# Batched matmul on one core: the seventh of eight output groups stored by two engines, in strided and uneven transfers

## The chip, the core and the metric

The kernel runs on one core of one Trainium2 chip. The metric is the device time of one execution in microseconds, as a median over runs. A profile of one execution stands beside it; its span goes from the first to the last instruction.

## The reference

```python
def setup_inputs():
    batch, dim_i, dim_j, dim_k = 32, 256, 512, 384
    ...  # x: [32, 256, 512] float32, y: [32, 512, 384] float32, normal draws

def reference(x, y):
    return np.einsum('bij,bjk->bik', x, y).astype(np.float32)
```

So there are 32 independent products of a 256x512 by a 512x384 matrix. x has 16.8 MB, y 25.2 MB, the output 12.6 MB.

## The kernel before

The batch is worked in N = 8 groups of Q = 4 matrices. On chip a group lies on all 128 partitions: matrix g has partitions 32g to 32g+31, and each partition holds R = 8 consecutive rows of x and of the output. Below, "row" means such a partition row of the output: 8 x 384 float32 = 12,288 bytes, contiguous in memory on both sides, 128 of them to a group. A group is computed in NE = 2 halves (the first and last four of the eight matrix rows of each partition).

The engines share the work of a group like this.

- SyncE (`sp`) issues every DMA. First the loads: `load_y` (L73) and `load_x` (L69) bring a group of y (3,072 KB) or x (2,048 KB) into one of two buffers; for groups 2 to 7 each load waits until GpSimd has converted the group two before it. Then the stores, all through `store` (L96): groups 0 to 4 in one DMA, groups 5 and 6 in a second, group 7 in a third. All outputs stay in `o_sb`, which has room for all eight groups, so no computation waits for a store.
- GpSimd (`po`) converts x and y to float16: `round_x` (L126), `round_y` (L136). Its last conversions are those of group 7. After them it waits for SyncE's `s_sp` and clears the semaphores.
- VectorE (`v`) transposes 32x32 blocks of the converted x (L156) and copies five of sixteen result blocks of each half from PSUM to `o_sb` (L165).
- TensorE (`te`) multiplies (L217), in four row groups of the array.
- ScalarE (`a_`) copies the other eleven result blocks of each half (L165).

The store part of SyncE's program:

```python
    sp.wait_ge(s_pe, chunk_done(JOINED, NE - 1, 0))
    store(0, JOINED)                 # groups 0 to 4
    sp.wait_ge(s_pe, chunk_done(N - 1, NE - 1, 0))
    store(JOINED, N - 1)             # groups 5 and 6
    sp.wait_ge(s_act, NE)
    sp.wait_ge(s_dve, NE)
    store(N - 1, N)                  # group 7
```

`s_pe` is counted up by TensorE; `chunk_done(n, e, a)` is its value when chunk a of half e of group n has been multiplied. That of the last half of group 7 can only be reached when the results of group 6 have been copied out, so the second store is safe there. The last lines of the program wait until all stores have landed.

Of the kernel before, what the change touches and what calls it, by code (L numbers as in the profile page):

```python
# [10 lines left out]
P = 128  # L11
Q = 4
NE = 2
STEP = 4
STRAIGHT = 2
JOINED = 5
# [3 lines left out]
def kernel(  # L20
# [6 lines left out]
    nc = tc.nc  # L27
# [4 lines left out]
    PQ = P // Q  # L32
    R = I // PQ
# [3 lines left out]
    N = B // Q  # L37
    NC = T // STEP

    def sbuf(name, shape, dtype):  # L40
        return nc.alloc_sbuf_tensor(name, shape, dtype).ap()
# [3 lines left out]
    o_sb = sbuf("o_sb", [P, N, NE, H, K], F32)  # L45
# [6 lines left out]
    s_x = [nc.alloc_semaphore(f"s_x{n}") for n in range(N)]  # L52
    s_y = [nc.alloc_semaphore(f"s_y{n}") for n in range(N)]
    s_xt = nc.alloc_semaphore("s_xt")
    s_yr = nc.alloc_semaphore("s_yr")
    s_cast = nc.alloc_semaphore("s_cast")
    s_free = nc.alloc_semaphore("s_free")
    s_act = nc.alloc_semaphore("s_act")
    s_dve = nc.alloc_semaphore("s_dve")
    s_pe = nc.alloc_semaphore("s_pe")  # L60
    s_sp = nc.alloc_semaphore("s_sp")
    s_out = nc.alloc_semaphore("s_out")
    mine = s_x + s_y + [s_xt, s_yr, s_cast, s_free, s_act, s_dve, s_pe, s_sp]
    nums = sorted(s.num for s in mine)
    assert nums == list(range(nums[0], nums[-1] + 1)) and s_out.num == nums[-1] + 1

# [21 lines left out]
    def chunk_done(n, e, a):  # L88
        return (n * NE + e) * MARKS + (a + 1 if a < NC - 1 else MARKS)

    sp = nc.sync

    def store(first, last):
        groups = out[first * Q : last * Q].rearrange("(n g) (s f) k -> (g s) n f k", g=Q, s=PQ)
        src = o_sb[:, first:last].rearrange("p n e h k -> p n (e h) k")
        sp.dma_start(out=groups, in_=src).then_inc(s_out, 16)  # L96

    for n in range(2, N):
# [3 lines left out]
        load_y(n)  # L102
    sp.wait_ge(s_pe, chunk_done(JOINED, NE - 1, 0))
    store(0, JOINED)
    sp.wait_ge(s_pe, chunk_done(N - 1, NE - 1, 0))
    store(JOINED, N - 1)
    sp.wait_ge(s_act, NE)
    sp.wait_ge(s_dve, NE)
    store(N - 1, N)
    sp.sem_inc(s_sp, 1)  # L110
    sp.wait_op(s_out, 16 * 3, "sem-ge").then_inc(s_out, -16 * 3)

    def pieces(n):
        w = 1 if n in (0, N - 2, N - 1) else 2
        return [(a, a + w) for a in range(0, NC, w)]

    po = nc.gpsimd

    def round_x(n):
        po.wait_ge(s_x[n], 16)
        for e in range(NE):
            if n:
                po.wait_ge(s_free, max(2 * n - 2 + e, 1))
            po.tensor_copy(  # L126
                x_r[:, e], x_sb[n % 2][:, e * H : (e + 1) * H]
            ).then_inc(s_cast, 1)

    def round_y(n):  # L130
        po.wait_ge(s_y[n], 16)
        for a, b in pieces(n):
            if n:
                po.wait_ge(s_pe, chunk_done(n - 1, NE - 1, b - 1))
            s = slice(a * STEP, b * STEP)
            ins = po.tensor_copy(y_r[:, s], y_sb[n % 2][:, s])  # L136
            ins.then_inc(s_yr, b - a if b < NC else b - a + NC)
# [3 lines left out]
    for n in range(1, N):  # L141
        round_x(n)
        round_y(n)
    po.wait_ge(s_sp, 1)
    po.sem_clear(range(nums[0], nums[-1] + 1))

# [84 lines left out]
    with te.Fori(0, N):  # L231
        with te.Fori(0, NE) as e:
            take(s_act)
            take(s_dve)
            for t in range(T):
# [3 lines left out]
                for g in range(Q):  # L239
                    s = slice(g * PQ, (g + 1) * PQ)  # L240
# [40 lines left out]
```

## Time and profile before

| | |
|---|---|
| median of 3 runs | 131.91 us (131.77 to 132.49) |
| the profiled execution, its own time | 132.13 us |
| its span | 130.8 us |
| bytes moved | 54.55 MB, mean 417 GB/s over the span |
| busy: PE, DVE, ACT, POOL | 61.4, 82.7, 84.1, 74.2 us |
| DMA transfers issued | 19: 16 loads and 3 stores, all by SyncE |

The profile's page gives busy times of the five compute engines and, apart from them, what the core's 16 DMA engines did: a row with their mean busy share in 40 equal slices of the span, and the rate in each slice. A DMA is cut into packets, and each of the 16 engines works its own packets one after the other. In this kernel a packet of a store is one row of 12,288 bytes, and every DMA ends with one small packet on each engine, which counts up its semaphore. The trace names no engine for a packet.

### The profile page before, as it was taken

Reading aid. Unit: us, or ns where it says so; the run is one execution under the profiler, and the core shown is the slowest. Engines: PE = TensorE matmul, PEld = TensorE weight load, DVE = VectorE, ACT = ScalarE, POOL = GpSimd, SP = SyncE. Lnnn points to the kernel's source line nnn. Section 1 sums busy time; section 2 is a strip of 40 time slices with the busy share of each in tenths; the row PEclk is TensorE's granted clock in tenths of the full one; section 3 lists DMA queues with packets and bytes.
Section 4 is the critical chain, followed back from the end, with each engine's and each line's share of the span. In section 5 each row is a group of like instructions: output and inputs, shape, how many; then the busy total and the mean of one; then the engine's idle time right before and its main releaser. Section 6 shows DMA issues by size and latency. Waiting matters only on the chain. (4 is left out here: it accounts for less than half of the span.)

```text
span 130.8 us, 3199 instructions
## 1 busy us (share of the span) xinstructions
PE 61.4 (47%) x1024; PEld 46.7 (36%) x1024; DVE 82.7 (63%) x144; ACT 84.1 (64%) x178; POOL 74.2 (57%) x42
## 2 busy tenths in 40 slices
PE   0000009910992589089329905980975499100000
PEld 0000009800991566046129604970953236000000
DVE  0000036899379999985997997599999957920000
ACT  0400000599659989993998899399999957994000
POOL 0006991199929965992899459758973970000000
PEclk9999999995589689977986985599599959965555
DMA  5999999999999999999999999999999999999995
GB/s 120 451 396 441 421 431 451 443 408 428 451 413 421 438 443 401 436 436 443 423 458 398 443 408 466 398 418 436 463 398 408 427 438 425 436 428 421 425 440 248
DMA packets 3379, 54.55 MB, mean 417 GB/s; under 512 B 304, under 2 KB 304, under 8 KB 304
## 3 DMA queue, kind: packets, MB, share of 16 engines
q1 hardware_dynamic: 3376, 54.53, 98.1%
q14 instruction: 3, 0.02, 0.0%
HBM read 41.94 MB, written 12.58 MB: 417 GB/s over the span
## 5 line engine op out<-in xcount | busy, mean ns | idle before, releaser
L165 ACT COPY o_sb<-o_ps (+1 forms) x176 | 82.6, 469 | 31.7 <-PE o_ps L217 29.6
L217 PE MATMUL o_ps<-y_r,xt_sb 32*128 32x384 f16 x1024 | 61.4, 384 | 50.4 <-PEq L214 49.5
L217 PEld LDWEIGHTS o_ps<-y_r,xt_sb 32*128 32x128 f16 x1024 | 46.7, 107 | 64.6 <-issue 56.8
L156 DVE STREAM_TRANSPOSE xt_sb<-x_r 128x256 f32<-128x256 f32 x64 | 38.1, 626 | 30.9 <-POOL x_r L126 18.4
L136 POOL CAST y_r<-y_sb 128x1536 f16<-128x1536 f32 (+1 forms) x22 | 44.3, 2049 | 15.8 <-DMA y_sb<-in_y_dram 15.3
L165 DVE COPY o_sb<-o_ps 32x384 f32 (+1 forms) x80 | 44.6, 557 | 1.6
L126 POOL CAST x_r<-x_sb 128x2048 f16<-128x2048 f32 x16 | 30.2, 1893 | 16.8 <-DVE o_sb L165 12.1
L202 ACT ACT_TABLE_LOAD x1 | 1.3, 1283 | 3.4 <-PEq L78 3.4
L265 POOL MEMSET const-float32-0.0<- 128x1 f32 x1 | 0.1, 98 | 0.2 <-issue 0.2
L202 ACT COPY spare<-const-float32-0.0 1x1 f32<-1x1 f32 x1 | 0.2, 190 | 0.0
L265 POOL MEMSET const-bfloat16-1.0<- 128x1 bf16 x1 | 0.1, 101 | 0.0
L265 POOL MEMSET const-uint8-127<- 128x1 uint8 x1 | 0.1, 101 | 0.0
L265 POOL MEMSET const-float32-1.0<- 128x1 f32 x1 | 0.1, 98 | 0.0
## 6 DMA issues: line engine op xcount, KB each, us to landing
y_sb<-in_y_dram SPq DMA_DIRECT2D x8, 3072.0 KB, 16.8
x_sb<-in_x_dram SPq DMA_DIRECT2D x8, 2048.0 KB, 17.0
out_dram<-o_sb SPq DMA_DIRECT2D x1, 7680.0 KB, 33.9
out_dram<-o_sb SPq DMA_DIRECT2D x1, 3072.0 KB, 17.3
out_dram<-o_sb SPq DMA_DIRECT2D x1, 1536.0 KB, 11.5
```

Of the source, the lines that this page charges most:

```text
L126: po.tensor_copy(x_r[:, e], x_sb[n % 2][:, e * H : (e + 1) * H]).then_inc(s_cast, 1)
L136: ins = po.tensor_copy(y_r[:, s], y_sb[n % 2][:, s])
L156: v.transpose(xt_w[:, w], words[:, e, w]).then_inc(s_xt, 1)
L165: ins = copy(o_sb[g * PQ : (g + 1) * PQ, n, e, h], o_ps[h * PQ : (h + 1) * PQ, e * Q + g, :K],)
L202: a_.copy(spare, nc.const_aps.tensor(0.0, [1, 1], F32))
L217: return te.add_instruction(mybir.InstMatmult(name=nc.get_next_instruction_name(), start_tensor_calc=start, stop_tensor_calc=stop, tile_si ...
L265: nc = _bacc.Bacc("TRN2", target_bir_lowering=False, num_devices=1)
```

## The change

Group 6 is no longer stored together with group 5. Group 5 gets a DMA of its own. Of group 6's 128 rows, SyncE stores 112 in three DMAs: every second row (64 rows), every fourth from row 1 (32 rows), every eighth from row 3 (16 rows). The other 16 rows, 7, 15, ... 127, are stored by GpSimd, in five DMAs, after its last conversion and after the same wait on `s_pe` that SyncE has. GpSimd's transfers are cut across the rows: some take matrix row 0 alone of each partition (1,536 bytes), some the matrix rows 1 to 7 (10,752 bytes).

| GpSimd's transfer | rows | matrix rows of each | bytes of each |
|---|---|---|---|
| first | 7 to 39 (5) | 0 | 1,536 |
| second | 47 to 127 (11) | 1 to 7 | 10,752 |
| third | 47 to 79 (5) | 0 | 1,536 |
| fourth | 7 to 39 (5) | 1 to 7 | 10,752 |
| fifth | 87 to 127 (6) | 0 | 1,536 |

SyncE waits for these five by a semaphore of their own, `s_few`, after it has issued the store of group 7. Computation is as before.

```diff
+    s_few = nc.alloc_semaphore("s_few")
...
+    def store_rows(eng, sem, n, first, step, f0=0, f1=R, rows=P):
+        dst = out[n * Q : (n + 1) * Q].rearrange("g (s f) k -> (g s) f k", s=PQ)
+        src = o_sb[:, n].rearrange("p e h k -> p (e h) k")
+        p = slice(first, min(first + rows * step, P), step)
+        eng.dma_start(out=dst[p, f0:f1], in_=src[p, f0:f1]).then_inc(sem, 16)
...
     sp.wait_ge(s_pe, chunk_done(N - 1, NE - 1, 0))
-    store(JOINED, N - 1)
+    store(JOINED, N - 2)
+    store_rows(sp, s_out, N - 2, 0, 2)
+    store_rows(sp, s_out, N - 2, 1, 4)
+    store_rows(sp, s_out, N - 2, 3, 8)
     sp.wait_ge(s_act, NE)
     sp.wait_ge(s_dve, NE)
     store(N - 1, N)
+    sp.wait_ge(s_few, 16 * 5)
     sp.sem_inc(s_sp, 1)
-    sp.wait_op(s_out, 16 * 3, "sem-ge").then_inc(s_out, -16 * 3)
+    sp.wait_op(s_out, 16 * 6, "sem-ge").then_inc(s_out, -16 * 6)
...
     for n in range(1, N):
         round_x(n)
         round_y(n)
+
+    po.wait_ge(s_pe, chunk_done(N - 1, NE - 1, 0))
+    store_rows(po, s_few, N - 2, 7, 8, 0, 1, 5)
+    store_rows(po, s_few, N - 2, 47, 8, 1, R, 11)
+    store_rows(po, s_few, N - 2, 47, 8, 0, 1, 5)
+    store_rows(po, s_few, N - 2, 7, 8, 1, R, 5)
+    store_rows(po, s_few, N - 2, 87, 8, 0, 1, 6)
     po.wait_ge(s_sp, 1)
```

More of the change, by code (lines that the diff above doesn't have):

```diff
@@ L61 @@
     s_sp = nc.alloc_semaphore("s_sp")
+    s_few = nc.alloc_semaphore("s_few")
     s_out = nc.alloc_semaphore("s_out")
-    mine = s_x + s_y + [s_xt, s_yr, s_cast, s_free, s_act, s_dve, s_pe, s_sp]
+    mine = s_x + s_y + [s_xt, s_yr, s_cast, s_free, s_act, s_dve, s_pe, s_sp, s_few]
     nums = sorted(s.num for s in mine)
```

## The prediction

> **What bounds the kernel now.** I read the page first, its time slices above all.
>
> ```profile
> span 130.8 us, 3199 instructions
> PE 61.4 (47%) x1024; PEld 46.7 (36%) x1024; DVE 82.7 (63%) x144; ACT 84.1 (64%) x178; POOL 74.2 (57%) x42
> DMA  5999999999999999999999999999999999999995
> DMA packets 3379, 54.55 MB, mean 417 GB/s; under 512 B 304, under 2 KB 304, under 8 KB 304
> q1 hardware_dynamic: 3376, 54.53, 98.1%
> q14 instruction: 3, 0.02, 0.0%
> ```
>
> No compute engine is busy for two thirds of the span, while the 16 DMA engines are busy in every slice but the first and the last, and 98.1% in all. So the bytes set the time. The row of queue 1 also counts packets: 304 small ones, which is 19 DMAs with one for each of 16 engines, and 3,072 large ones. Does a wait of SyncE ever leave the engines empty? The queue's waits and the issues answer that.
>
> ```profile
> SPq L96 <- PE o_ps L217: 24.9, 2, 23.5
> SPq L111 <- SPq L111: 11.1, 1, 11.1
> 109.82 9.80 SPq L96 DMA_DIRECT2D out_dram<-o_sb  x2
> L96 SPq DMA_DIRECT2D out_dram<-o_sb x3: 345/390/403, 85.9 to 119.3; - x3
> out_dram<-o_sb SPq DMA_DIRECT2D x1, 7680.0 KB, 33.9
> out_dram<-o_sb SPq DMA_DIRECT2D x1, 3072.0 KB, 17.3
> out_dram<-o_sb SPq DMA_DIRECT2D x1, 1536.0 KB, 11.5
> ```
>
> The first store is issued at 85.9 us and lands 33.9 us later, at 119.8. The second goes out at 109.82, ten microseconds before that; the third at 119.27, and lands at 130.8, the end. Each is in the queue before the one ahead of it is done, so the engines never run dry; SyncE's waits cost nothing, and its last wait, 11.1 us, is for the bytes.
>
> Next the rate, by stage, from the windows.
>
> ```profile
> core 0: us, PE busy (x) PEld busy (x) DVE busy (x) ACT busy (x) POOL busy (x), PEclk, DMA share, GB/s
> 4.00:97.00 93.00, 50.41 (x835) 40.76 (x835) 67.15 (x117) 64.01 (x137) 66.37 (x33) 0.85 1.01 431
> 109.80:119.00 9.20, 1.94 (x46) 1.19 (x37) 5.21 (x10) 8.96 (x20) 0.00 (x0) 0.79 1.01 431
> 119.00:127.00 8.00, 0.00 (x0) 0.00 (x0) 0.00 (x0) 0.25 (x1) 0.00 (x0) 0.50 0.99 424
> ```
>
> Loads and stores run at the same 431 GB/s, 26.9 GB/s for each of 16 engines. One row of 12,288 bytes therefore holds an engine for 12,288 / 26.9 = 456 ns. That is the unit of all that follows. Nothing in the change removes a byte, so only the last stretch, where engines finish one by one, can give anything back. Here are the DMA packets from 129.0 us on, in 40 slices of 50 ns.
>
> ```profile
> DMA  9550005959000000500000000000000000000000
> GB/s 983 246 246 0 0 0 246 738 246 492 0 0 0 0 0 0 246 0 0 0 0 0 0 0 0 0 0 0 0 0 0 0 0 0 0 0 0 0 0 0
> DMA packets 30, 0.17 MB, mean 86 GB/s; under 512 B 16, under 2 KB 16, under 8 KB 16
> ```
>
> A packet is entered where it starts, and 246 GB/s for 50 ns is 12.3 KB, one row. So the numbers are counts: 4, 1, 1 rows start from 129.00 to 129.15, then 1, 3, 1, 2 from 129.30 to 129.50, and a single one at 129.80 to 129.85. (30 packets are these 14 rows and 16 small ones.) Each engine repeats every 456 ns. The seven after 129.30 belong to seven engines; the six before belong to six others or to two of these seven and four others, since one that starts at 129.00 starts again at 129.46. The two at the end of the second cluster (129.45 to 129.50) are such repeats, so four engines end near 129.5, the other five had started their last row before 129.0 and end by 129.46 (I take 129.3; all 16 small packets lie after 129.0, so none ended earlier), six end near 129.85, and one ends at 129.83 + 0.456 = 130.3, alone. The time from there to the landing at 130.8 is the same for all. So the kernel's end is set by one of 16 DMA engines, which is one row late.
>
> The mean end is (5 x 129.3 + 4 x 129.53 + 6 x 129.86 + 130.3) / 16 = 129.63. Perfect sharing would end 0.67 us earlier. This is the ceiling of any gain: 0.5% of the profiled time. About 0.5% is also what a measurement of this kernel can tell from no change (the three runs lie within 131.77 to 132.49).
>
> **The change part by part.** *Group 5 split off, and three strided DMAs.* SyncE issues four DMAs from 109.82 instead of one: at 390 ns each until 111.4, eight microseconds ahead of 119.27, when it issues group 7. Queued behind them is only that store, and it waits for the last copies anyway. Cost on SyncE: 0. If that cover were gone, 3 x 0.39 = 1.2 us.
>
> *Small packets.* Three more DMAs by SyncE and five by GpSimd add up to 8 small packets per engine. The two windows at 431 GB/s hold one DMA end in 9.2 us and some 15 in 93 us; within the rounding of the rate (0.5 in 431, 0.1 us of 93) the 15 cost at most 0.2 us, so one costs at most 14 ns. Eight: 0 to 0.11 us. I take 0.05.
>
> *GpSimd's issues.* Is GpSimd free?
>
> ```profile
> 104.15 2.88 POOL L136 CAST y_r<-y_sb 128x1536 f16<-128x1536 f32 x2
> L136 POOL CAST y_r<-y_sb x22: 1462/1467/2747, 10.9 to 105.6; 128x1536 f16<-128x1536 f32 x12, 128x3072 f16<-128x3072 f32 x10
> ```
>
> Its last conversion ends at 107.03, so its new wait ends at 109.8 as SyncE's does; behind it stands only the clearing of semaphores, which nobody waits for until the end. No DMA by GpSimd is in this trace. Its issue lies between SyncE's 0.345 us and its own longest instruction, 2.75 us: five take 1.7 to 13.7 us and end at 111.5 to 123.5. I take 1 us each, nearer to the row of the same operation, so 115. The 16 rows they move then still have 14 us. It would delay the end only if one transfer took (129.0 - 109.8) / 5 = 3.8 us. Cost 0. [...]
>
> *Who carries which bytes.* SyncE's 64, 32 and 16 rows divide by 16: 4 + 2 + 1 = 7 rows for each engine, where group 6 had 8. GpSimd's 16 rows would be one for each engine if spread evenly, but they are cut in 5, 11, 5, 5 and 6. The trace shows no such transfer. Bounds: an engine that gets none ends 0.456 us earlier; one that is first in all five transfers gets 3 x 1,536 + 2 x 10,752 = 26,112 bytes, 2.13 rows, and ends 1.13 x 0.456 = 0.51 us later. If the five transfers instead follow one another around the engines (5 + 11 and 5 + 5 + 6 are 16 each), five engines get 2 x 1,536 = 3,072 bytes and lose 0.75 row, 0.34 us; five get 2 x 10,752 bytes and gain 0.34 us; six keep 12,288 bytes. I take this second form for the size, since its three groups of 5, 5 and 6 are near the groups that the tail shows (5 early, 4 between, 7 late), and it lies between the bounds.
>
> [...]
>
> *Does that move the end?* The late engine ends at 130.3, the next at 129.93 (the last of the six, which starts its last row by 129.5). If the late one is relieved, the end falls by 0.34; if it is one of the six, it stays; if it is loaded, +0.34. With 0.05 for small packets: -0.29, +0.05, +0.39. Five engines end together early, and loading those costs nothing; then the late one is among the relieved or the untouched. I take the middle of these two, -0.1. Against the profiled 132.13 us that is 132.0; against the median 131.91, from which it is 0.22 away as runs differ, 131.8. The forecast case reaches from 131.6 (late engine relieved) to 132.2 (untouched, dearer small packets, part of a conflict below).
>
> **The rivals.** *Strided rows make engines get into each other's way.* Every DMA of the trace covers all 128 partitions, so no row shows what 16 engines do on every second, fourth or eighth partition. If two engines then read from the same part of the on-chip memory, and each row took 912 ns instead of 456, the seven rows of group 6 would cost 7 x 0.456 = 3.2 us on every engine: 135.1. If only the 16-row transfer is hit, 0.46 us; the 32 and 16 rows, 1.4 us; so 132.4 to 135.1. It decides from the point at which more than one of the seven rows doubles. For it: all engines run at the same 26.9 GB/s in loads and stores, as if something of a fixed width behind each were the limit. Against it: a stride of 2, 4 or 8 still reaches all of the partitions' range, and the limit may be the engine itself. 0.27 for over 0.5%.
>
> [...]
>
> *The wrong engines are loaded* (the change does not do what an uneven split is for): the late engine gets 0.34 to 0.51 us more, 132.3 to 132.5. For it: nothing in the trace says which engine is late; against it, 11 of 16 are not loaded. 0.14, and still within 0.5%.
>
> *GpSimd's DMAs disturb the engines*: a second queue makes each engine change over several times, or an issue takes over 3.8 us. Two to five stalls of about a row's time, 0.3 us, come to 0.7 to 1.5 us: 132.6 to 133.4. Against it: the three packets of queue 14 in the rows above went between those of queue 1 and the share stayed at 98.1%. 0.06.
>
> *All engines end together*, and the runs without a profile have a later straggler than this one: 0.67 us or more gained, 131.2 or less. A step of 0.34 us can't level a spread of 1 us. 0.06.
>
> **How the numbers follow.** Forecast 0.47, wrong engines 0.14: within 0.5%, 0.61. Strided conflicts 0.27 and disturbance 0.06: slower, 0.33. Faster 0.06. The range begins at 131.3, below the forecast's own 131.6 by half the 0.7 us over which the three runs lie, rounded to 0.3, and goes up to 134.0: it takes in the disturbance and all partial conflicts and leaves out the near full doubling (0.12) and most of the faster case (0.05).
>
> **What would show it.** Right: rows of group 6 still take 456 ns, so the rate stays near 431 GB/s from 109.8 to 127 us; group 7's store is issued at 119.3; GpSimd's issues end by 116 us and its rows land long before the end; the last rows start closer together than 129.0 to 129.85. Wrong: a stretch of several microseconds after 119 us at well under 431 GB/s (strided conflict), a slice between packets of the two queues with engines idle (disturbance), or two engines or more a row later than the others (wrong engines).

## The result: 0.6% slower, and the tail of one engine grew

The changed kernel took 132.77 us (median of 8 runs, 132.46 to 133.17), the kernel before 131.97 us beside it; the ratio is 1.0061, with a 95% interval of 1.0041 to 1.0081. So it is slower by 0.8 us, where 131.8 us was forecast. The profiled execution is one of the longer ones, 133.17 us with a span of 131.8 us.

Its page, the rows that answer those shown of before:

```profile
span 131.8 us, 3207 instructions
PE 65.4 (50%) x1024; PEld 52.5 (40%) x1024; DVE 82.4 (63%) x144; ACT 84.1 (64%) x178; POOL 76.7 (58%) x47
DMA  5999999999999999999999999999999999999993
DMA packets 3571, 54.55 MB, mean 414 GB/s; under 512 B 480, under 2 KB 496, under 8 KB 496
q1 hardware_dynamic: 3408, 54.33, 97.2%
q0 software_dynamic: 160, 0.20, 0.4%
q14 instruction: 3, 0.02, 0.0%
```

The bytes are the same, and the engines are as full as before, except in the last slice: 3 tenths instead of 5. A queue 0 has come in, with GpSimd's 0.20 MB. SyncE's waits and the issues, from the waits of the queue, GpSimd's timeline and the instructions that write the output:

```profile
SPq L124 <- SPq L124: 11.0, 1, 11.0
SPq L120 <- DVE o_sb L185: 1.8, 1, 1.8
SPq L123 <- DMA out_dram<-o_sb: 1.3, 1, 1.3
110.50 2.67 POOL L100 DMA_DIRECT2D out_dram<-o_sb  x5 [3.09 <-PE o_ps L237]
L100 POOL DMA_DIRECT2D out_dram<-o_sb x5: 518/518/636, 110.5 to 112.6; - x5
L105 SPq DMA_DIRECT2D out_dram<-o_sb x3: 337/350/407, 87.2 to 119.2; - x3
L100 SPq DMA_DIRECT2D out_dram<-o_sb x3: 758/870/949, 110.6 to 112.3; - x3
```

GpSimd's five issues end at 113.2, SyncE's strided ones at 113.3, and group 7's store still goes out at 119.2. SyncE's wait for GpSimd's rows takes 1.3 us and ends 11.0 us before the end. So nothing was issued late. The rates by stage, from the windows (columns as in the prediction; the last is GB/s):

```profile
109.80:119.00 9.20, 2.33 (x57) 1.30 (x48) 5.08 (x10) 8.96 (x20) 2.67 (x5) 0.91 1.01 426
119.00:127.00 8.00, 0.00 (x0) 0.00 (x0) 0.00 (x0) 0.13 (x1) 0.00 (x0) 0.50 1.02 428
127.00:129.00 2.00, 0.00 (x0) 0.00 (x0) 0.00 (x0) 0.00 (x0) 0.00 (x0) 0.50 0.98 418
```

Where GpSimd's rows move, the rate is 426 instead of 431 GB/s, which is 0.1 us of these 9.2; from 119 to 127 us it is 428, where it was 424 before. Most of the difference stands in the tail. The DMA packets from 129.0 us, in slices of 50 ns, where 246 GB/s is one row that starts:

```profile
DMA  9099590009559050009505500005500000000500
GB/s 737 0 492 737 246 492 0 0 0 737 246 246 983 0 246 0 0 0 492 246 0 246 246 0 0 0 0 246 246 0 0 0 0 0 0 0 0 246 0 0
DMA packets 44, 0.36 MB, mean 178 GB/s; under 512 B 15, under 2 KB 15, under 8 KB 15
```

Before, one row started after 129.5. Here eight rows start from 129.9 on; two of them at 130.35 to 130.45, one of whose engines starts yet another at 130.87 and ends at 131.33, where the last small packet stands. From that packet to the end of the span it is 0.5 us, as before from 130.30 to 130.8. One engine is now two rows or more behind most of the others. In this execution the last row starts 1.03 us later than before (130.87 against 129.85), a little more than the 0.8 us of the medians.

### The profile page after: what moved, and what is told of

Its sections match the earlier page's. It is cut to its first block, busy times and chain, and to the rows that moved or that the text cites. A ratio compares the mean times of both kernels' runs of the same rounds, so it can differ in the third digit from the quotient of the medians.

```text
span 131.8 us, 3207 instructions
## 1 busy us (share of the span) xinstructions
PE 65.4 (50%) x1024; PEld 52.5 (40%) x1024; DVE 82.4 (63%) x144; ACT 84.1 (64%) x178; POOL 76.7 (58%) x47
## 3 DMA queue, kind: packets, MB, share of 16 engines
q1 hardware_dynamic: 3408, 54.33, 97.2%
## 5 line engine op out<-in xcount | busy, mean ns | idle before, releaser
L237 PE MATMUL o_ps<-y_r,xt_sb 32*128 32x384 f16 x1024 | 65.4, 406 | 46.7 <-PEq L234 43.5
L237 PEld LDWEIGHTS o_ps<-y_r,xt_sb 32*128 32x128 f16 x1024 | 52.5, 113 | 59.2 <-issue 52.0
L100 POOL DMA_DIRECT2D out_dram<-o_sb x5 | 2.7, 542 | 3.1 <-PE o_ps L237 3.1
```

The lines of the kernel that those rows point to most:

```text
L100: eng.dma_start(out=dst[p, f0:f1], in_=src[p, f0:f1]).then_inc(sem, 16)
L237: return te.add_instruction(mybir.InstMatmult(name=nc.get_next_instruction_name(), start_tensor_calc=start, stop_tensor_calc=stop, tile_si ...
```

## The experiments

Theory A: GpSimd's transfers all begin at the same engine. Then the first five engines, counted from that one, carry 3 x 1,536 + 2 x 10,752 bytes of group 6's last rows, 2.13 rows, and the last five carry none; and the engine that ends last is among the first five. Theory B: strided rows make engines get in each other's way. Theory C: GpSimd's queue with its many small packets costs the time. Each kernel is the changed one with the edit shown, timed beside the kernel before; the counts that SyncE waits for follow the number of DMAs and are not shown.

**Five even transfers.** The same 16 rows, the same number of transfers.

```diff
-    store_rows(po, s_few, N - 2, 7, 8, 0, 1, 5)   # and the other four, of 11, 5, 5, 6 rows
+    store_rows(po, s_few, N - 2, 7, 8, 0, 1, 16)
+    store_rows(po, s_few, N - 2, 7, 8, 1, 3, 16)
+    store_rows(po, s_few, N - 2, 7, 8, 3, 5, 16)
+    store_rows(po, s_few, N - 2, 7, 8, 5, 7, 16)
+    store_rows(po, s_few, N - 2, 7, 8, 7, 8, 16)
```

> Still five transfers by GpSimd of the same 16 rows, but each has all 16 rows and a part of their length, so that every DMA engine gets one row (12,288 bytes). Uneven loads (theory A: the five transfers all begin at the same engine, five engines get 2.13 rows and end 0.51 us later): most of the 0.8 us goes, ratio to before 1.000 to 1.003. Strided rows in each other's way (B) or GpSimd's queue and its many small packets (C): ratio stays at 1.005 to 1.007.

132.32 us, ratio 1.0015 (0.9999 to 1.003). Three quarters of the loss are gone with the unevenness alone. Its packets on the page also tell how a transfer is dealt out to the engines:

```profile
DMA packets 3571, 54.55 MB, mean 416 GB/s; under 512 B 432, under 2 KB 464, under 8 KB 512
q0 software_dynamic: 160, 0.20, 0.4%
```

Here queue 0's 160 packets are 80 pieces of rows and 80 small ones, one for each transfer and engine. In the changed kernel they are 32 pieces and 128 small ones (432 + 48 = 480 under 512 bytes in all). The 48 more are as many as the transfers leave engines without a row: 11 + 5 + 11 + 11 + 10 = 48. That is what comes out if each of these transfers of 5, 6 or 11 rows uses as many engines as it has rows, one row each. Which ones, the next kernels show.

**SyncE stores all of group 6; and GpSimd stores its rows in one transfer.**

```diff
     store_rows(sp, s_out, N - 2, 3, 8)
+    store_rows(sp, s_out, N - 2, 7, 8)          # first kernel; nothing by GpSimd
...
+    store_rows(po, s_few, N - 2, 7, 8)          # second kernel, instead of the five
```

> SyncE stores all of group 6 in four strided DMAs (64, 32, 16, 16 rows), GpSimd stores nothing. A: ratio 1.000 to 1.002. B: 1.006 or more, since a strided 16-row DMA is added. C: 1.000 to 1.002.

> GpSimd stores its 16 rows in one DMA of whole rows: one row for each engine, one fifth of GpSimd's transfers. A: 1.000 to 1.002. B: 1.005 to 1.007. C: a fifth to a half of the 0.6%, 1.001 to 1.003; below five_even by 0.3% or more.

132.10 us, ratio 1.001 (0.9993 to 1.0027), and 132.12 us, ratio 1.000 (0.9985 to 1.0014). Neither the strided DMAs with two 16-row ones among them nor GpSimd's queue with one transfer accounts for 0.6%.

**The five uneven transfers, issued by SyncE.**

```diff
     store_rows(sp, s_out, N - 2, 3, 8)
+    store_rows(sp, s_out, N - 2, 7, 8, 0, 1, 5)      # and none of them by GpSimd
+    store_rows(sp, s_out, N - 2, 47, 8, 1, R, 11)
+    store_rows(sp, s_out, N - 2, 47, 8, 0, 1, 5)
+    store_rows(sp, s_out, N - 2, 7, 8, 1, R, 5)
+    store_rows(sp, s_out, N - 2, 87, 8, 0, 1, 6)
```

> The five uneven transfers as in the changed kernel, but issued by SyncE after its three strided ones; GpSimd issues nothing. A (uneven loads make the loss): if SyncE's transfers also take the first engines, the ratio is that of the changed kernel less the cost of GpSimd's queue (1.0015, the five even ones): 1.004 to 1.006. C (GpSimd's queue makes it): 1.000 to 1.002.

133.01 us, ratio 1.0079 (1.0059 to 1.0098). The whole loss is there without GpSimd, so C falls as its cause. It is more than the 1.004 to 1.006 that A had said; the interval overlaps that of the changed kernel, and a difference between the two is not shown. The page counts 384 small packets here, 32 more than the other 22 DMAs have with 16 each (352), and 5 + 11 + 5 + 5 + 6 is 32, which fits one engine for each row with SyncE's transfers, too; so these, unlike the DMAs of the kernel before, do not have a small packet on each of the 16 engines. The tail, from 130.0 us in slices of 50 ns:

```profile
DMA  0090505000000000500000000000000000000000
GB/s 0 0 492 0 246 0 246 0 0 0 0 0 0 0 0 0 246 0 0 0 0 0 0 0 0 0 0 0 0 0 0 0 0 0 0 0 0 0 0 0
```

Four engines start a row at 130.1 to 130.35, one of them again at 130.8; of the kernel before, no row starts after 129.85.

**Which engines: transfers of four rows, and one row more for the first four, three or two.**

```diff
-    (the five transfers of 5, 11, 5, 5 and 6 rows)
+    store_rows(po, s_few, N - 2, f, 8, 0, R, 4)      # fours: f = 7, 39, 71, 103
...
+    store_rows(po, s_few, N - 2, 7, 8, 0, R, 12)     # low4; low3: 13 and 3 rows; low2: 14 and 2
+    store_rows(po, s_few, N - 2, 103, 8, 0, R, 4)
```

> GpSimd stores its 16 rows in four transfers of four whole rows. A: if each transfer begins at the same engine, four engines get four rows each, three more than their share, 3 x 0.456 = 1.37 us: ratio 1.008 to 1.013, and the tail shows four engines three rows late. If the transfers went round the engines, every engine would get one row and the ratio would be 1.000 to 1.003. B: 1.005 to 1.007. C: 1.004 to 1.006 (four transfers for five).

> GpSimd stores 12 whole rows in one transfer and 4 in another: by theory A the first four engines get one row more than their share, the last four one row less. If the late engine is one of the first four, +0.456 us over the single even transfer (1.000): 1.0025 to 1.004. If it is not: 1.000 to 1.0015. In the changed kernel the five loaded ones held it, so the first is expected, unless it is the fifth.

> GpSimd stores 13 whole rows in one transfer and 3 in another: the first three engines get one row more than their share. With four loaded engines the ratio was 1.0027, with two 1.0008, so the late engine is the third or the fourth. If the third: 1.0025 to 1.004 here. If the fourth: 1.000 to 1.0015.

> GpSimd stores 14 whole rows in one transfer and 2 in another: the first two engines get one row more than their share. If the late engine is one of these two: 1.0025 to 1.004. If not: 1.000 to 1.0015. Nothing yet says which; half and half.

| kernel | rows above their share, if each transfer begins at the same engine | us | ratio (95%) |
|---|---|---|---|
| one transfer of 16 | none | 132.12 | 1.000 (0.9985 to 1.0014) |
| 14 and 2 | first two: 1 | 132.18 | 1.0008 (0.9995 to 1.002) |
| 13 and 3 | first three: 1 | 132.27 | 1.0022 (1.0009 to 1.0035) |
| 12 and 4 | first four: 1 | 132.36 | 1.0027 (1.0015 to 1.0039) |
| four of 4 | first four: 3 | 133.04 | 1.0075 (1.0048 to 1.0102) |

Four transfers of four would load every engine with one row if they went round; they cost 0.75%, or 0.99 us, a little under the 1.0 to 1.7 us (1.008 to 1.013) that A had said. Their tail, from 130.0 us:

```profile
DMA  0550000550050000090000000000000000000000
GB/s 0 246 246 0 0 0 0 246 246 0 0 246 0 0 0 0 0 492 0 0 0 0 0 0 0 0 0 0 0 0 0 0 0 0 0 0 0 0 0 0
```

Three engines start a row at 130.35 to 130.6, and two of these three start one more at 130.85 to 130.9. The trace also shows GpSimd's rows as they move, by the packets of queue 0 (packets, MB, share of 16 engines). All four transfers were issued by 112.1 us. Here are four windows of 60 ns, from 114.34, 115.72, 117.10 and 118.47 us:

```profile
q0 software_dynamic: 2, 0.02, 95.8%
q0 software_dynamic: 4, 0.02, 97.7%
q0 software_dynamic: 4, 0.02, 97.7%
q0 software_dynamic: 2, 0.02, 95.8%
```

In each, two rows (0.02 MB) of one transfer start, 1.38 us after two rows of the transfer before it; the other two rows of each transfer do so from 114.96, 116.34, 117.71 and 119.09 us. By an estimate from the row's time, 1.38 us is three rows of 0.46: the engine's own row, and two of SyncE's in turn, though no view shows these two on that engine. An engine that had no row of the transfer before, as when they go round, would by the same estimate have only these two to wait for, some 0.92 us. So, by this estimate, the four transfers use the same four engines, and the tail and the time (1.0075) agree: each transfer begins at the same engine. No view names that engine.

Which of the loaded engines ends last is less sure. One row more on four engines costs 0.36 us (0.27% of 132), near the row's 0.456 us; a row more on an engine that ends just ahead of the last (129.93 against 130.3 us before) would have cost 0.09. This points to the last engine being among the first four. For three engines the interval overlaps that of four, and for two it overlaps both that of four and that of the one transfer; three also ran on another chip than four and two. So which one of the four it is stays open.

**What strides cost.** SyncE stores group 6 alone, as rows 0 to 63 and 64 to 127, as even and odd rows, or in eight DMAs of every eighth row.

```diff
+    store_rows(sp, s_out, N - 2, 0, 1, 0, R, 64)     # halves
+    store_rows(sp, s_out, N - 2, 64, 1, 0, R, 64)
...
+    store_rows(sp, s_out, N - 2, 0, 2)               # evenodd
+    store_rows(sp, s_out, N - 2, 1, 2)
...
+    for f in range(8):                               # eighths
+        store_rows(sp, s_out, N - 2, f, 8)
```

> SyncE stores group 6 in two DMAs of 64 neighbouring rows, 0 to 63 and 64 to 127, instead of strided ones; GpSimd stores nothing. If 16 engines on half of the partitions share half of the memory's width, each of 8 rows takes 912 ns: 8 x 0.456 = 3.65 us more, ratio 1.02 to 1.03, and the rate falls to about 215 GB/s for 7 us after 122.9 us. If the width belongs to the engine: 1.000 to 1.001.

> SyncE stores group 6 in two DMAs of 64 rows, the even and the odd ones; GpSimd stores nothing. Same count and sizes as with rows 0 to 63 and 64 to 127 (ratio 1.0224). If neighbouring rows of one half share a width and alternate rows keep each engine on its own (B holds for halves, not for a stride of 2): 1.000 to 1.001. If any DMA of 64 rows is hit: 1.02.

> SyncE stores group 6 in eight DMAs of 16 rows, every eighth row from 0, 1, ... 7; GpSimd stores nothing. The changed kernel has one such DMA by SyncE, and packets of up to 1.5 us were seen near it, on few engines. If a 16-row DMA puts engines two by two on the same part (B for a stride of 8): up to 8 rows doubled, ratio 1.005 to 1.028, the rate well under 400 GB/s from 122.9 to 126.6 us. If not: 1.001 to 1.003 for the six more DMAs.

Ratios 1.0224 (1.0198 to 1.0249), 0.9997 (0.9988 to 1.0006) and 1.0174 (1.016 to 1.0188). In each kernel group 6's rows move at about 122.9 to 126.5 us. Here is that window in each (last column GB/s). The kernel before, and the same line for the even and odd rows:

```profile
122.90:126.50 3.60, 0.00 (x0) 0.00 (x0) 0.00 (x0) 0.00 (x0) 0.00 (x0) 0.50 1.02 434
```

The changed kernel:

```profile
122.90:126.50 3.60, 0.00 (x0) 0.00 (x0) 0.00 (x0) 0.00 (x0) 0.00 (x0) 0.50 1.00 413
```

The halves:

```profile
122.90:126.50 3.60, 0.00 (x0) 0.00 (x0) 0.00 (x0) 0.00 (x0) 0.00 (x0) 0.50 1.08 317
```

The eighths:

```profile
122.90:126.50 3.60, 0.00 (x0) 0.00 (x0) 0.00 (x0) 0.00 (x0) 0.00 (x0) 0.50 1.06 300
```

So B is a real effect, but not for a stride of 2. With 64 neighbouring rows, or with eight DMAs of 16 rows in steps of eight, the engines fall to 317 and 300 GB/s while they are busy all the time (shares 1.08 and 1.06): a row takes longer, as an estimate 16 x 12,288 bytes at these rates, 0.62 and 0.66 us, instead of 0.456. What makes it longer, no view shows.

The changed kernel has one 16-row DMA by SyncE, and 413 GB/s in this window. Its rows there take longer in a few cases: where the expectation speaks of up to 1.5 us, the longest of this window in the trace, from 125.45 us, takes 1.30 us. This does not explain its loss. The kernel in which SyncE stores all of group 6 has two of them, shows the same 413 GB/s, and takes 132.10 us; and over the longer window of 119 to 127 us the changed kernel moves no less than the kernel before (428 and 424 GB/s).

None of these kernels beats the one before; the even and odd rows equal it.

## Why the prediction was wrong, point by point

- *What bounds the kernel* was right: bytes through 16 engines (98.1% of their span before, 97.2% and 0.4% with the change), and the end set by one late engine (it ends at 130.3 us before, at 131.33 with the change). Nothing that the change did to issues or waits mattered.
- *The issues* were right in result. GpSimd's took 0.54 us each on average, not 1; SyncE's strided ones 0.76 to 0.95 us, not 0.39. Both ended six microseconds ahead of need.
- *Small packets* were mis-sized in number: 128 by GpSimd and 48 by SyncE, 11 per engine, where up to 8 were reckoned. The price is bounded: five even transfers against one, 0.15% or 0.2 us, with intervals that overlap.
- *Who carries which bytes* is the step that failed. I had both forms, the transfers that follow one another around the engines and those that all begin anew, and took the first because its groups of 5, 5 and 6 resembled the tail's groups. The four transfers of four show the second. The size that was worked out for the second, 0.51 us for an engine that is first in all five, was near: uneven against even cost 1.0061 - 1.0015, 0.46% or 0.61 us, and the two intervals leave some 0.3 us either way. No run shows the 0.34 us of the first form, with which the sum was made. By the tails, the packets of queue 0 and the ratios here (1.0075 for four transfers of four), GpSimd's short transfers began anew each time, and SyncE's transfers of 5, 6 and 11 rows lose as much (1.0079 against 1.0061).
- *Does that move the end?* failed with it. I took the loaded five for the five that end early, from counts alone, so that loading them cost nothing and the term came out at -0.1 us. The tail's counts name no engine, so this was a guess in the dress of a reading. The change loads the same five engines with each transfer, and the end moved by +0.8 us; the engine that ends last is, by the run with 12 and 4 rows, most likely one of them.
- *The rival "wrong engines"* is what happened; its sign, two engines or more a row later than the others, is in the tail. It was priced at 132.3 to 132.5, so within 0.5%, and had 0.14. Measured 132.77: 0.6 of the 0.8 us is the unevenness, and the other 0.2 us is what five even transfers still cost against the kernel before (1.0015, with an interval from 0.9999). That part is not told from zero, and its cause stays open; the sum had 0.05 us for small packets. That 132.77 lies inside the stated range of 131.3 to 134.0 us is luck as far as the sum goes: the range went up so far for strided conflicts and a disturbance by GpSimd, and neither made the loss.
- *The rival "strided rows"* was priced at up to 3.2 us, since I could not tell which stride is hit: 64 rows at a stride of 2 are free (0.9997). Eight DMAs of 16 rows at a stride of 8 cost 2.3 us, but one or two of them, as in the changed kernel and in the one where SyncE stores all of group 6, show no loss beyond the noise, where 0.46 us was priced for one. What decides is not shown: in the same window 64 neighbouring rows moved at 317 GB/s, every eighth row at 300, even and odd rows at 434. As an estimate from a row of 912 ns, twice 456, the halves would cost 3.65 us; measured 2.24%, 3.0 us.
- *GpSimd's DMAs disturb the engines* did not occur: with one transfer the ratio is 1.000. The stall of 0.3 us that it was priced with was an assumption; no run shows one.

## What to carry to other kernels

This kernel is bound by transfers, and its end belonged to one DMA engine, whose last row started alone at 129.85 us before and at 130.87 with the change; so the sum must be made for each engine, not for the total. A transfer with fewer rows than the 16 engines is an uneven load, and here such transfers loaded the same engines each time, by GpSimd as the packets 1.38 us apart suggest and by SyncE as the equal loss does (1.0061 and 1.0079); so splitting into odd pieces moved bytes toward them and never away. Before loads are shifted to level a tail, find out which engines are late, by giving a known few of them one unit more and seeing whether the end moves.

## What the runs showed of the hardware that was not expected

- In the kernel before, one engine ends 0.37 us after the next, and most likely it is among the first four: a row more on these (0.456 us) moved the end by 0.36 us. Why it is late is open.
- Two DMAs of 64 neighbouring partitions each cost 3.0 us for 1.5 MB, two of alternate ones nothing (0.9997); eight DMAs of every eighth partition cost 2.3 us.
- SyncE's issue of a strided DMA takes 0.76 to 0.95 us in the changed kernel, of one over 64 neighbouring partitions 0.81 to 0.93 us, of a plain one over all 128 partitions 0.34 to 0.41 us in these two kernels.
- Five transfers by GpSimd with 48 places left without a row have 48 small packets more (128 against 80): as it seems, an engine that gets no row handles two small packets instead of one.
